# Thirteen gate projections of the first feed-forward as seven products on half the tokens instead of eight

## Chip, cores and metric

One NeuronCore of one Trainium2 chip runs the whole program in one launch. The metric is device microseconds of one execution, the median of three. Everything is in 32-bit floats; where a matmul operand is split into two parts, the parts are `float32r`, the engine's reduced 32-bit type.

## The reference

One inference step of one decoder layer on 256 prompt tokens and 8 x 8 sample tokens, 320 tokens together, with a model width of 2048:

```python
x += 0.5 * swiglu(rmsnorm(x, ln_ffa), w_ffa_in, w_ffa_out)   # first feed-forward, D_FF = 5632
x += token_mixer(rmsnorm(x, ln_mix), ...)                    # mLSTM and dilated attention
x += 0.5 * swiglu(rmsnorm(x, ln_ffb), w_ffb_in, w_ffb_out)   # second feed-forward
y = rmsnorm(x, ln_f)

def swiglu(x, w_in, w_out):
    gate, up = jnp.split(x @ w_in, 2, axis=-1)
    return (jax.nn.silu(gate) * up) @ w_out
```

The change concerns `x @ w_in` of the first feed-forward, gate half. New keys, values and recurrent states are outputs too.

## The kernel before

Channels lie on the 128 partitions and tokens in the free dimension, so a matmul has a 128 x 128 piece of the weights as stationary operand and a channel tile of 128 x 320 (NT = 320 tokens) as moving operand. For accuracy, both operands are split into a high and a low part, and each product is three matmuls: high weight by high data (`xh,hi`), high weight by low data (`xl,hi`), low weight by high data (`xh,lo`). Each of these matmuls loads its own weights first.

The matmuls are cut into jobs, one for each 256 output channels, and a job into chunks of up to four channel tiles. A chunk's weights (128 x 4 x 256, 512 KB) come by one DMA into a `raw` tile (5 buffers); ScalarE copies `raw` to `hi` (L239), VectorE writes `lo` = `raw` - `hi` (L112 is the helper through which all of VectorE's instructions pass); `hi` and `lo` have 3 buffers each (HLB = 3). A full chunk is 4 tiles x 2 column halves x 3 = 24 matmuls (L147 is the helper that issues them).

The program's order is written out by hand, per chunk, at its head in `run_job`: postponed work first (`run_later`: what `later(...)` was given at the chunk before), then in a job's first chunk the evacuation of the job before (`flush_evac`), then `split_upto(ci + HLB)`, which splits the weights of the chunk two places ahead into the buffers that the chunk before this one used, then one step of the background generators (`step`), the loads, and last the chunk's matmuls. Each engine takes its instructions strictly in this order.

The first feed-forward has 22 pairs of jobs, in blocks of 6, 6, 5 and 5. Each pair is a gate job (16 channel tiles, 4 chunks, 96 matmuls) and an up job of the same size. After a block come 8 jobs that multiply by `w_ffa_out`. A gate job's PSUM tile is evacuated in the up job's first chunk: VectorE multiplies by `rstd` into `gt`, ScalarE applies SiLU, GpSimd multiplies by `rstd` again (L472). An up job's PSUM tile is evacuated in the next job's first chunk: VectorE multiplies it by `gt` into `hf`, ScalarE copies that to `hh`, VectorE writes `hl`; these are the moving operands of the `w_ffa_out` jobs. `fg` tiles (2 banks, 2 buffers) hold the PSUM of the jobs, `bg` tiles (1 bank, 4 buffers) the small work. The first gate and up job run in a start-up routine of their own, with the same 192 matmuls.

Of the kernel before, what the change touches and what calls it, by code (L numbers as in the profile page):

```python
# [9 lines left out]
F32 = mybir.dt.float32  # L10
# [112 lines left out]
def decoder_kernel(tc, I, O, K):  # L123
# [54 lines left out]
    def run_later(force=False):  # L178
        run_queue(later_q, force)
# [38 lines left out]
    def split_upto(n):  # L218
        while st["split"] < min(n, len(chunks)):
            i = st["split"]  # L220
            load_upto(i + 1)
            src, nk, kind = chunks[i]
            hi = wp.tile([128, 4, 256], F32R, tag="hi", bufs=HLB, name="hi")
            lo = wp.tile([128, 4, 256], F32R, tag="lo", bufs=HLB, name="lo")
            t = raw.pop(i)
            if kind == "mif":
                r = t.rearrange("p a b -> p (a b)")[:, :128].rearrange("p (k c) -> p k c", k=16)
                pair = []
                for a, w in enumerate((hi, lo)):
                    G.memset(w.bitcast(F32), 0.0)  # L230
                    x = w.rearrange("p a b -> p (a b)").rearrange("p (k c) -> p k c", k=8)
                    for o, s in ((0, 0), (32, 4)):
                        rk = r[:, 8 * a:8 * a + 8, s:s + 4]
                        S.copy(x[:, :, o:o + 4], rk)
                        V.tensor_tensor(x[:, :, o + 64:o + 68], rk, x[:, :, o:o + 4].bitcast(F32), op=OP.subtract)
                    pair.append(x)
                wh[i], wl[i] = pair, None
            else:
                S.copy(hi[:, :nk], t[:, :nk])  # L239
                V.tensor_tensor(lo[:, :nk], t[:, :nk], hi[:, :nk].bitcast(F32), op=OP.subtract)  # L240
                wh[i], wl[i] = hi, lo
            st["split"] += 1
# [17 lines left out]
                k += nk  # L260
        jobs.append((cs, nkt, mov, evac, kind, setup))

    fgps = [0]

    def fg_tile():
        return pp.tile([128, 2, 512], F32, tag="fg", bufs=2, name="fg")
# [7 lines left out]
    def flush_evac():  # L274
        if pending:
            evac, ps = pending.pop(0)
            g = evac(ps)
            if g is not None:
                try:
                    next(g)  # L280
                    every.append(g)
                except StopIteration:
                    pass

    def run_job(job):
        cs, nkt, mov, evac, kind, setup = job
        third = cs[0][0] == 8
        ps = [bg_tile(), bg_tile()] if third else fg_tile()
        for n, (ci, k0, nk) in enumerate(cs):
            us = CHUNK_US + extra[0]  # L290
            V.next_chunk(us)
            moved[1] = max(0.0, moved[1] + moved[0] - us * MB_PER_US)
            extra[0] = moved[0] = 0.0
            run_later()
            now = list(every)
            if n == 0 and setup is not None:
                setup()
            if n == (3 if third else 0) or ci == 13:
                flush_evac()
            split_upto(ci + HLB)  # L300
            run_queue(soon_q)
            if tick[0] % 2 == 0:
                step(even)
                if moved[1] < 3.4:
                    step(slow)
            else:
                step(odd)
            tick[0] += 1
            step(every, now)
            while fill and V.has_room(CHUNK_US + extra[0]):  # L310
                if next(fill[0], True):
                    break
            load_upto(ci + HLB + RAWB)
            h, l = wh.pop(ci), wl.pop(ci)
            if kind == "mif":
                for k in range(nk):
                    for n2, x in enumerate(mov(k0 + k)):
                        mm(ps[:, 0, 0:NT], h[k // 8][:, k % 8], x, start=k == 0 and n2 == 0, stop=k == nk - 1 and n2 == 1)
                continue
            for m in range(2):  # L320
                for k in range(nk):
                    if ci == 10 and m == 0 and k == 2:
                        rstd_now(True)
                    xh, xl = mov(k0 + k)
                    a, b = h[:, k, m * 128:(m + 1) * 128], l[:, k, m * 128:(m + 1) * 128]
                    out = ps[m][:, 0:NT] if third else ps[:, m, 0:NT]
                    first, last = k0 + k == 0, k0 + k == nkt - 1
                    mm(out, a, xh, start=first, stop=False)
                    mm(out, a, xl, start=False, stop=False)
                    mm(out, b, xh, start=False, stop=last)  # L330
        pending.append((evac, ps))

    def drain(n=100000):
        while (every or even or odd or slow) and n > 0:
# [125 lines left out]
        S.copy(h, xe)  # L460
        V.tensor_tensor(l, xe, h.bitcast(F32), op=OP.subtract)

    def ff_jobs(w_in, w_out, get, last_evac, first_setup=None):
        f0 = 0
        for bi, nb in enumerate(FF_BLOCKS):
            for m in range(0, nb, 2):
                def gate_evac(ps):
                    p = get()
                    gt = p.tile([128, 2, NT], F32, tag="ft", bufs=4, name="gt")
                    times_rstd(gt, ps)  # L470
                    S.activation(gt, gt, AF.Silu)  # L471
                    G.tensor_tensor(gt, gt, bcast(rstd, 2), op=OP.mult)  # L472
                    state["gt"] = gt

                def up_evac(ps, m=m):
                    p = get()
                    h = p.tile([128, 2, NT], F32, tag="ft", bufs=4, name="hf")
                    V.tensor_tensor(h, ps[:, :, 0:NT], state["gt"], op=OP.mult)
                    hh = p.tile([128, 2, NT], F32R, tag="h", bufs=state["hb"], name="hh")
                    hl = p.tile([128, 2, NT], F32R, tag="h", bufs=state["hb"], name="hl")  # L480
                    split(h, hh, hl)
                    H_H[m // 2], H_L[m // 2] = hh, hl

                add_job(w_in, 0, 16, (f0 + m) * 128, mov_x, gate_evac,
                        setup=first_setup if (bi == 0 and m == 0) else None)
# [21 lines left out]

    state["hb"] = 12
    pool_box = {"p": fp}
    ff_jobs(I["w_ffa_in"], I["w_ffa_out"], lambda: pool_box["p"], ffa_last)  # L510
    n_ffa = len(jobs)


# [1221 lines left out]
    spawn(init_tables(), even)  # L1735
    run_start()
    spawn(first_sumsq())
    for job in jobs[2:-1]:
        run_job(job)
    run_last(jobs[-1])  # L1740
# [129 lines left out]
```

## Time and profile before

| | |
|---|---|
| median of three runs | 2663.82 us (2663.71 to 2666.66) |
| the profiled execution's own time | 2665.36 us |
| its span | 2663.4 us |
| TensorE matmul busy / weight load busy | 99% / 99% of the span, 21296 instructions each |
| VectorE, ScalarE, GpSimd busy | 57%, 43%, 6% |
| granted TensorE clock | 0.998 of full speed |

A row of the profile's groups reads: line, engine, operation, written tile <- read tiles, shapes, count | busy time in all, mean ns of one | idle time of the engine before them and who ended it. PE is the matmul queue, PEld the weight loads, which the profile records as separate instructions; matmuls overlap, so their durations are longer than the distance from one to the next. DVE is VectorE, ACT ScalarE, POOL GpSimd. A row of the timeline reads: start, duration of the merged instructions, then the same names.

### The profile page before, as it was taken

The numbers are of one execution on the slowest core, as the hardware profiler recorded it, in microseconds if no ns is written. First come the engines' busy times: TensorE is split into PE (matmuls) and PEld (weight loads), VectorE is DVE, ScalarE is ACT, GpSimd is POOL, SyncE is SP. The second block draws the span as 40 slices with busy tenths as digits, with TensorE's granted clock in tenths as the row PEclk, the third lists the DMA queues.
The fourth block names the chain that finished last, engine by engine and source line by source line (L and its number), as shares of the span: only waits on it lengthen the run. The fifth ranks groups of instructions, "written<-read, shape, count | busy, mean of one in ns | idle before, by whom it ended". The sixth has DMA issues, their size and how long they took to land.

```text
span 2663.4 us, 50949 instructions
## 1 busy us (share of the span) xinstructions
PE 2647.3 (99%) x21296; PEld 2629.3 (99%) x21296; DVE 1518.3 (57%) x1962; ACT 1136.1 (43%) x1879; POOL 147.5 (6%) x171
## 2 busy tenths in 40 slices
PE   9999999999999999999999999999999999999998
PEld 9999999999999999999999999999999999999998
DVE  6444444444446576777766656655545555554445
ACT  6333333333334455555544445443333433433334
POOL 0000000000000000111101000000000000000000
PEclk9999999999999999999999999999999999999999
DMA  6544455445546778899999876566666565555444
GB/s 238 161 164 163 163 159 165 159 155 163 168 159 186 248 245 296 310 343 324 339 375 355 319 257 228 192 201 201 195 203 194 176 214 187 194 168 174 160 152 132
DMA packets 202290, 571.55 MB, mean 215 GB/s; under 512 B 23488, under 2 KB 65096, under 8 KB 202060
## 3 DMA queue, kind: packets, MB, share of 16 engines
q1 hardware_dynamic: 201340, 566.99, 63.4%
q8 instruction: 166, 2.72, 0.4%
q10 hardware_dynamic: 720, 1.31, 0.1%
q14 instruction: 64, 0.52, 0.1%
HBM read 535.45 MB, written 32.78 MB: 213 GB/s over the span
## 4 chain that ended last, share of the span: by engine, by line
PE 98%; DMA 1%; DVE 0%; ACT 0%; SPq 0%; issue 0%; DVEq 0%; ACTq 0%
PE fg L147 93%; PE bg L147 4%; DMA vt<-in_old_v_dram 1%; PE bg L357 1%; DMA fk<-in_far_k_dram 0%; DMA x<-in_x_t_dram 0%; DVE x L112 0%; DVE lo L112 0%; SPq L139 0%; DVE rows L112 0%; ACT xh L1653 0%; ACT hi L239 0%; ACT lg L1747 0%; ACT hi L1643 0%; ACT s L604 0%
## 5 line engine op out<-in xcount | busy, mean ns | idle before, releaser
L112 DVE TENSOR_TENSOR lo<-raw,hi 128x1024 fp32r<-128x1024 f32 (+2 forms) x794 | 966.4, 1222 | 847.6 <-ACT hi L239 827.6
L147 PE MATMUL fg<-xh,hi 128*128 128x320 f32 x4200 | 1258.4, 301 | 1.4 <-ACT hi L1643 1.4
L147 PE MATMUL fg<-xh,lo 128*128 128x320 f32 x4200 | 1248.3, 299 | 0.3 <-DVE lo L112 0.3
L147 PE MATMUL fg<-xl,hi 128*128 128x320 f32 x4200 | 1248.3, 299 | 0.0
L239 ACT CAST hi<-raw 128x1024 fp32r<-128x1024 f32 (+1 forms) x776 | 793.2, 1026 | 1062.6 <-PE fg L147 899.6
L147 PEld LDWEIGHTS fg<-xh,hi 128*128 128x128 f32 x4200 | 791.5, 189 | 7.4 <-issue 2.9
L147 PEld LDWEIGHTS fg<-xl,hi 128*128 128x128 f32 x4200 | 791.8, 189 | 0.6
L147 PEld LDWEIGHTS fg<-xh,lo 128*128 128x128 f32 x4200 | 791.4, 189 | 0.6 <-DVE lo L112 0.6
L147 PE MATMUL fg<-hh,hi 128*128 128x320 f32 x1408 | 421.4, 299 | 0.0
L147 PE MATMUL fg<-hl,hi 128*128 128x320 f32 x1408 | 421.0, 299 | 0.0
L147 PE MATMUL fg<-hh,lo 128*128 128x320 f32 x1408 | 421.0, 299 | 0.0
L147 PEld LDWEIGHTS fg<-hh,hi 128*128 128x128 f32 x1408 | 266.1, 189 | 0.3
L147 PEld LDWEIGHTS fg<-hl,hi 128*128 128x128 f32 x1408 | 266.1, 189 | 0.1
L147 PEld LDWEIGHTS fg<-hh,lo 128*128 128x128 f32 x1408 | 266.1, 189 | 0.0
L472 POOL TENSOR_TENSOR gt<-gt,rstd 128x640 f32<-128x640 f32 x44 | 68.2, 1549 | 1651.5 <-ACT gt L471 1651.5
L147 PE MATMUL fg<-bh,hi 128*128 128x320 f32 x512 | 153.3, 299 | 0.0
L147 PE MATMUL fg<-bl,hi 128*128 128x320 f32 x512 | 153.1, 299 | 0.0
L147 PE MATMUL fg<-bh,lo 128*128 128x320 f32 x512 | 153.1, 299 | 0.0
L147 PEld LDWEIGHTS fg<-bh,hi 128*128 128x128 f32 x512 | 96.8, 189 | 0.2 <-issue 0.2
L147 PEld LDWEIGHTS fg<-bl,hi 128*128 128x128 f32 x512 | 96.8, 189 | 0.0
L147 PEld LDWEIGHTS fg<-bh,lo 128*128 128x128 f32 x512 | 96.8, 189 | 0.0
L460 ACT CAST hh<-hf 128x640 fp32r<-128x640 f32 x44 | 34.8, 790 | 143.5 <-DVE hf L112 143.5
(264 smaller groups left out, 1414.7 us busy)
## 6 DMA issues: line engine op xcount, KB each, us to landing
raw<-in_w_in_dram SPq DMA_DIRECT2D x176, 512.0 KB
raw<-in_w_ffb_in_dram SPq DMA_DIRECT2D x176, 512.0 KB
raw<-in_w_ffa_in_dram SPq DMA_DIRECT2D x171, 512.0 KB
raw<-in_w_ffa_out_dram SPq DMA_DIRECT2D x80, 512.0 KB
vt<-in_old_v_dram SPq DMA_DIRECT2D x80, 512.0 KB
raw<-in_w_ffb_out_dram SPq DMA_DIRECT2D x80, 512.0 KB
fk<-in_far_k_dram SPq DMA_DIRECT2D x48, 512.0 KB
nk<-in_near_k_dram SPq DMA_DIRECT2D x32, 512.0 KB
```

The lines of the kernel that those rows point to most:

```text
L112: return fn(*a, **k)
L147: T.matmul(out, a, b, start=start, stop=stop, **kw)
L239: S.copy(hi[:, :nk], t[:, :nk])
L357: T.transpose(out, in_, ident[:k, :k])
L460: S.copy(h, xe)
L472: G.tensor_tensor(gt, gt, bcast(rstd, 2), op=OP.mult)
```

## The change

In pairs 3, 4, 6, 7, 9, 10, 12, 13, 15, 16, 18, 19 and 21 (counted from 0) the gate and the up job become one job of kind `pair`, whose eight chunks alternate gate, up, gate, up. The up chunks compute what they did, into two `bg` tiles. A gate chunk is computed by a seven-product scheme for 2 x 2 block matrices: two channel tiles by two column halves of the weights, times two channel tiles by two halves of the tokens (HT = 160). A block takes 7 products of 128 x 128 by 128 x 160, each again three matmuls, so 42 matmuls a chunk and 168 a gate job. Four of the seven weight operands are sums and differences of weight tiles: VectorE forms them from `raw` (tiles `f` and `g`, named `sums`), ScalarE and VectorE split them into `sh` and `sl`. Four of the seven moving operands are sums of token halves; `token_sums` forms them once (`th`, `tl`), as a background generator during pairs 1 and 2. The seven products accumulate in an `fg` tile and a `bg` tile; `gate_evac7` and `join7` add them up into `gt`. The head of a chunk becomes a function (`head`), the plain matmuls another (`plain`); both are the code of `run_job` moved, and `split_upto` gets a branch for kind `s`.

```diff
+            elif kind == "s":
+                sh, sl = (pool_box["p"].tile([128, 4, 2, 128], F32R, tag=g, bufs=2, name=g) for g in ("sh", "sl"))
+                f, g = (t_tile(F32, "sums").rearrange("p m n -> p (m n)")[:, 0:512].rearrange("p (q b n) -> p q b n", q=2, b=2)
+                        for _ in range(2))
+                S.copy(hi, t)
+                V.tensor_tensor(f.rearrange("p q b n -> p b q n"), raw_ap(t, 128, [[t.ap[0][0], 128], [512, 2], [0, 2], [1, 128]]),
+                                raw_ap(t, 0, [[t.ap[0][0], 128], [512, 2], [384, 2], [1, 128]]), op=OP.add)
+                V.tensor_tensor(g[:, 0], f[:, 1], t[:, 0::2, 0:128], op=OP.add)
+                V.tensor_tensor(g[:, 1], g[:, 0], t[:, 1::2, 0:128], op=OP.add)
+                for n, x in ((0, f), (2, g)):
+                    S.copy(sh[:, n:n + 2], x)
+                for k in (slice(0, 4), slice(1, 4, 2)):
+                    c = slice(0, 128) if k.start == 0 else slice(128, 256)
+                    V.tensor_tensor(lo[:, k, c], t[:, k, c], hi[:, k, c].bitcast(F32), op=OP.subtract)
+                for n, x in ((0, f), (2, g)):
+                    V.tensor_tensor(sl[:, n:n + 2], x, sh[:, n:n + 2].bitcast(F32), op=OP.subtract)
+                wh[i], wl[i] = (hi, sh), (lo, sl)
...
+    def add_pair(w, k_all, c0, c1, mov, evac0, evac1):
+        cs = []
+        for k in range(0, k_all, 4):
+            for a, c in enumerate((c0, c1)):
+                cs.append((len(chunks), k, a))
+                chunks.append((wsrc(w, k, 4, c), 4, "w" if a else "s"))
+        jobs.append((cs, k_all, mov, (evac0, evac1), "pair", None))
...
+    HT = NT // 2
+
+    def run_pair(job):
+        cs, nkt, mov, evac, kind, setup = job
+        f = fg_tile()
+        g = bg_tile()
+        acc = [g[:, 0:HT] if b == 0 else f[:, b - 1, c * HT:(c + 1) * HT] for b, _, c in
+               ((0, 0, 0), (1, 0, 0), (1, 0, 2), (2, 0, 0), (2, 0, 1), (1, 0, 1), (2, 0, 2))]
+        opens = (0, 1, 3)
+        u = None
+        for n, (ci, k0, a) in enumerate(cs):
+            hl = head(ci, 1 if n not in (0, 7) else 0)
+            if a:
+                if u is None:
+                    u = [bg_tile(), bg_tile()]
+                plain([t[:, 0:NT] for t in u], hl, mov, k0, 4, nkt)
+            else:
+                assert state["sums"]
+                (h, sh), (l, sl) = hl
+                for b in range(2):
+                    j = (k0 + 2 * b) // 2
+                    x = [tuple(t[j][:, kk].rearrange("p (j i) -> p i j", j=2)[:, 80 * c:80 * c + 80] for t in (XH, XL))
+                         for kk, c in ((0, 0), (1, 0), (1, 1))]
+                    y = [tuple(t[j][:, q // 2].rearrange("p (j i) -> p i j", j=2)[:, 80 * (q % 2):80 * (q % 2) + 80]
+                               for t in (TH, TL)) for q in range(4)]
+                    k = 2 * b
+                    w = [(t[:, k, 0:128], t[:, k + 1, 0:128], None, t[:, k + 1, 128:256]) for t in (h, l)]
+                    v = [[t[:, q, b] for q in range(4)] for t in (sh, sl)]
+                    left = [(w[0][0], w[1][0]), (w[0][1], w[1][1]), (v[0][3], v[1][3]), (w[0][3], w[1][3]),
+                            (v[0][1], v[1][1]), (v[0][2], v[1][2]), (v[0][0], v[1][0])]
+                    right = [x[0], x[1], x[2], y[3], y[0], y[1], y[2]]
+                    first, last = k0 + b == 0, k0 + k == nkt - 2
+                    for i, ((p, q), (xh, xl)) in enumerate(zip(left, right)):
+                        mm(acc[i], p, xh, start=first and i in opens, stop=False)
+                        mm(acc[i], p, xl, start=False, stop=False)
+                        mm(acc[i], q, xh, start=False, stop=last and b and i in (0, 5, 6))
+            if n == 6:
+                pending.append((evac[0], (f, g)))
+        pending.append((evac[1], u))
...
+    TH, TL = {}, {}
+
+    def join7(o, f):
+        o = o.rearrange("p m n -> p (m n)").rearrange("p (s n) -> p s n", s=4)
+        p, q = (f[:, b, 0:3 * HT].rearrange("p (s n) -> p s n", s=3) for b in range(2))
+        p34 = raw_ap(f, 2 * HT, [[f.ap[0][0], 128], [512 - 2 * HT, 2], [1, HT]])
+        V.tensor_tensor(o[:, 0::3], o[:, 0::3], p[:, 0:2], op=OP.add)
+        V.tensor_tensor(o[:, 1], o[:, 3], q[:, 1], op=OP.subtract)
+        V.tensor_tensor(o[:, 2], q[:, 2], o[:, 3], op=OP.subtract)
+        V.tensor_tensor(o[:, 3], o[:, 2], q[:, 1], op=OP.add)
+        V.tensor_tensor(o[:, 1:3], o[:, 1:3], p34, op=OP.add)
+
+    def token_sums(gcol):
+        for j in range(8):
+            x, t = t_tile(F32, "tx"), t_tile(F32, "tf")
+            for m in range(2):
+                S.activation(x[:, m], X[j][:, m], AF.Copy, scale=gv[:, gcol + 2 * j + m:gcol + 2 * j + m + 1])
+            t4 = t.rearrange("p m n -> p (m n)").rearrange("p (s n) -> p s n", s=4)
+            a, b = ([x[:, m, c * HT:(c + 1) * HT] for c in range(2)] for m in range(2))
+            yield
+            V.tensor_tensor(t4[:, 0], a[1], a[0], op=OP.subtract)
+            V.tensor_tensor(t4[:, 2], a[1], b[1], op=OP.subtract)
+            V.tensor_tensor(t4[:, 1], t4[:, 0], b[1], op=OP.subtract)
+            V.tensor_tensor(t4[:, 3], t4[:, 1], b[0], op=OP.add)
+            TH[j], TL[j] = (pool_box["p"].tile([128, 2, NT], F32R, tag="tt", bufs=16, name=n) for n in ("th", "tl"))
+            src = [t4[:, 2 * i:2 * i + 2].rearrange("p b (i j) -> p j b i", j=2) for i in range(2)]
+            hi, lo = ([u[:, i].rearrange("p (j b i) -> p j b i", j=2, b=2) for i in range(2)] for u in (TH[j], TL[j]))
+            for i in range(2):
+                S.copy(hi[i], src[i])
+            yield
+            for i in range(2):
+                V.tensor_tensor(lo[i], src[i], hi[i].bitcast(F32), op=OP.subtract)
+        state["sums"] = True
...
+                def gate_evac7(ps):
+                    gt = get().tile([128, 2, NT], F32, tag="ft", bufs=4, name="gt")
+                    S.copy(gt.rearrange("p m n -> p (m n)").rearrange("p (s n) -> p s n", s=4)[:, 0::3], bcast(ps[1][:, 0:HT], 2))
+
+                    def rest():
+                        join7(gt, ps[0])
+                        V.tensor_tensor(gt, gt, bcast(rstd, 2), op=OP.mult)
+                        S.activation(gt, gt, AF.Silu)
+                        G.tensor_tensor(gt, gt, bcast(rstd, 2), op=OP.mult)
+                        state["gt"] = gt
+
+                    later(rest)
+
                 def up_evac(ps, m=m):
                     p = get()
                     h = p.tile([128, 2, NT], F32, tag="ft", bufs=4, name="hf")
-                    V.tensor_tensor(h, ps[:, :, 0:NT], state["gt"], op=OP.mult)
+                    if isinstance(ps, list):
+                        for i in range(2):
+                            V.tensor_tensor(h[:, i], ps[i][:, 0:NT], state["gt"][:, i], op=OP.mult)
+                    else:
+                        V.tensor_tensor(h, ps[:, :, 0:NT], state["gt"], op=OP.mult)
                     hh = p.tile([128, 2, NT], F32R, tag="h", bufs=state["hb"], name="hh")
                     hl = p.tile([128, 2, NT], F32R, tag="h", bufs=state["hb"], name="hl")
                     split(h, hh, hl)
                     H_H[m // 2], H_L[m // 2] = hh, hl
 
+                if seven(f0 + m):
+                    add_pair(w_in, 16, (f0 + m) * 128, DFF + (f0 + m) * 128, mov_x, gate_evac7, up_evac)
+                    continue
...
-    ff_jobs(I["w_ffa_in"], I["w_ffa_out"], lambda: pool_box["p"], ffa_last)
+    ff_jobs(I["w_ffa_in"], I["w_ffa_out"], lambda: pool_box["p"], ffa_last, seven=lambda m: m >= 6 and m // 2 % 3 != 2)
...
     spawn(first_sumsq())
+    spawn(token_sums(G_FFA))
```

On TensorE, the start of the gate job of pair 3. Before (`xh`, `xl`: the two parts of the moving data; `hi`, `lo`: of the weights; `fg`: PSUM):

```order
L147 MATMUL fg<-xh,hi 128x320 [waits Activation_49]
L147 MATMUL fg<-xl,hi 128x320
L147 MATMUL fg<-xh,lo 128x320 [waits DVE_49]
L147 MATMUL fg<-xh,hi 128x320
L147 MATMUL fg<-xl,hi 128x320
L147 MATMUL fg<-xh,lo 128x320
```

After (`sh`, `sl`: the parts of the weight sums; `th`, `tl`: of the token sums):

```order
L147 MATMUL bg<-xh,hi 128x160 [waits Activation_49]
L147 MATMUL bg<-xl,hi 128x160
L147 MATMUL bg<-xh,lo 128x160 [waits DVE_49]
L147 MATMUL fg<-xh,hi 128x160 [waits PE_49]
L147 MATMUL fg<-xl,hi 128x160
L147 MATMUL fg<-xh,lo 128x160
L147 MATMUL fg<-xh,sh 128x160 [waits Activation_49]
L147 MATMUL fg<-xl,sh 128x160
L147 MATMUL fg<-xh,sl 128x160 [waits DVE_49]
L147 MATMUL fg<-th,hi 128x160
L147 MATMUL fg<-tl,hi 128x160
L147 MATMUL fg<-th,lo 128x160
```

The matmuls are half as wide and more; the third product also waits for `sh` and `sl`.

On VectorE, from the evacuation of a gate job to the first weights split after the up job. Before (`lo`: low part of a chunk's weights, one row a chunk):

```order
L112 TENSOR_TENSOR gt<-fg,rstd 128x640 [waits PE_49]
L112 TENSOR_TENSOR lo<-raw,hi 128x1024 [waits DMAHW4_49,DVE_49,Activation_49]
L112 TENSOR_TENSOR lo<-raw,hi 128x1024 [waits DVE_49,DMAHW5_49,PE_49,Activation_49]
L112 TENSOR_TENSOR lo<-raw,hi 128x1024 [waits DVE_49,DMAHW6_49,PE_49,Activation_49]
L112 TENSOR_TENSOR lo<-raw,hi 128x1024 [waits DMAHW7_49,PE_49,Activation_49]
L112 TENSOR_TENSOR hf<-fg,gt 128x640 [waits PE_49,Pool_49]
L112 TENSOR_TENSOR hl<-hf,hh 128x640 [waits Activation_49]
L112 TENSOR_TENSOR lo<-raw,hi 128x1024 [waits DMAHW0_49,Activation_49]
```

After, between pairs 3 and 4:

```order
L112 TENSOR_TENSOR gt<-gt,fg 128x2x160 [waits PE_49]
L112 TENSOR_TENSOR gt<-gt,fg 128x160 [waits DVE_49]
L112 TENSOR_TENSOR gt<-fg,gt 128x160
L112 TENSOR_TENSOR gt<-gt,fg 128x160 [waits DVE_49]
L112 TENSOR_TENSOR gt<-gt,fg 128x320 [waits DVE_49]
L112 TENSOR_TENSOR gt<-gt,rstd 128x640 [waits DVE_49]
L112 TENSOR_TENSOR hf<-bg,gt 128x320 [waits PE_49,Pool_49]
L112 TENSOR_TENSOR hf<-bg,gt 128x320 [waits PE_49]
L112 TENSOR_TENSOR hl<-hf,hh 128x640 [waits Activation_49]
L112 TENSOR_TENSOR sums<-raw 128x2x2x128 [waits DMAHW0_49]
L112 TENSOR_TENSOR sums<-sums,raw 128x256 [waits DVE_49] x2
L112 TENSOR_TENSOR lo<-raw,hi 128x4x128 [waits Activation_49]
```

Four chunks' splits stood between the making of `gt` and its use in `hf`; now none does, and the weights of the chunk two places on come behind both.

More of the change, by code (lines that the diff above doesn't have):

```diff
@@ L261, in add_job @@
         jobs.append((cs, nkt, mov, evac, kind, setup))
-    fgps = [0]
+    def add_pair(w, k_all, c0, c1, mov, evac0, evac1):
[5 more added lines that the diff above has]
+        jobs.append((cs, k_all, mov, (evac0, evac1), "pair", None))
     def fg_tile():
@@ L283, in flush_evac, with head, plain @@
                     pass
+    def head(ci, n, third=False, setup=None):
+        us = CHUNK_US + extra[0]
+        V.next_chunk(us)
+        moved[1] = max(0.0, moved[1] + moved[0] - us * MB_PER_US)
+        extra[0] = moved[0] = 0.0
+        run_later()
+        now = list(every)
+        if n == 0 and setup is not None:
+            setup()
+        if n == (3 if third else 0) or ci == 13:
+            flush_evac()
+        split_upto(ci + HLB)
+        run_queue(soon_q)
+        if tick[0] % 2 == 0:
+            step(even)
+            if moved[1] < 3.4:
+                step(slow)
+        else:
+            step(odd)
+        tick[0] += 1
+        step(every, now)
+        while fill and V.has_room(CHUNK_US + extra[0]):
+            if next(fill[0], True):
+                break
+        load_upto(ci + HLB + RAWB)
+        return wh.pop(ci), wl.pop(ci)
+    def plain(outs, hl, mov, k0, nk, nkt, at=None):
+        h, l = hl
+        for m in range(2):
+            for k in range(nk):
+                if at == (m, k):
+                    rstd_now(True)
+                xh, xl = mov(k0 + k)
+                a, b = h[:, k, m * 128:(m + 1) * 128], l[:, k, m * 128:(m + 1) * 128]
+                first, last = k0 + k == 0, k0 + k == nkt - 1
+                mm(outs[m], a, xh, start=first, stop=False)
+                mm(outs[m], a, xl, start=False, stop=False)
+                mm(outs[m], b, xh, start=False, stop=last)
     def run_job(job):
         cs, nkt, mov, evac, kind, setup = job
+        if kind == "pair":
+            run_pair(job)
+            return
         third = cs[0][0] == 8
@@ L289, in run_job @@
         for n, (ci, k0, nk) in enumerate(cs):
[L290 to L314, printed above, removed]
+            hl = head(ci, n, third, setup)
             if kind == "mif":
+                h, l = hl
                 for k in range(nk):
@@ L319, in run_job @@
                 continue
[L320 to L330, printed above, removed]
@@ L331, in run_job @@
-        pending.append((evac, ps))
+            outs = [ps[m][:, 0:NT] if third else ps[:, m, 0:NT] for m in range(2)]
+            plain(outs, hl, mov, k0, nk, nkt, (0, 2) if ci == 10 else None)
+        pending.append((evac, ps))
+    HT = NT // 2
[36 more added lines that the diff above has]
+        pending.append((evac[1], u))
@@ L461, in split, with ff_jobs @@
         V.tensor_tensor(l, xe, h.bitcast(F32), op=OP.subtract)
-    def ff_jobs(w_in, w_out, get, last_evac, first_setup=None):
+    TH, TL = {}, {}
[11 more added lines that the diff above has]
+            x, t = t_tile(F32, "tx"), t_tile(F32, "tf")
+            for m in range(2):
+                S.activation(x[:, m], X[j][:, m], AF.Copy, scale=gv[:, gcol + 2 * j + m:gcol + 2 * j + m + 1])
[15 more added lines that the diff above has]
+        state["sums"] = True
+    def ff_jobs(w_in, w_out, get, last_evac, first_setup=None, seven=lambda m: False):
         f0 = 0
@@ L477, in up_evac @@
                     h = p.tile([128, 2, NT], F32, tag="ft", bufs=4, name="hf")
-                    V.tensor_tensor(h, ps[:, :, 0:NT], state["gt"], op=OP.mult)
+                    if isinstance(ps, list):
+                        for i in range(2):
+                            V.tensor_tensor(h[:, i], ps[i][:, 0:NT], state["gt"][:, i], op=OP.mult)
+                    else:
+                        V.tensor_tensor(h, ps[:, :, 0:NT], state["gt"], op=OP.mult)
                     hh = p.tile([128, 2, NT], F32R, tag="h", bufs=state["hb"], name="hh")
```

## The prediction

> **What bounds the kernel now.** I read the page first, then the chain of work that ended last, then the groups of instructions by shape, then the timeline at a few places.
>
> ```profile
> span 2663.4 us, 50949 instructions
> PE 2647.3 (99%) x21296; PEld 2629.3 (99%) x21296; DVE 1518.3 (57%) x1962; ACT 1136.1 (43%) x1879; POOL 147.5 (6%) x171
> PE 98%; DMA 1%; DVE 0%; ACT 0%; SPq 0%; issue 0%; DVEq 0%; ACTq 0%
> ```
>
> TensorE is the bound from end to end. The chain by pieces gives its pace, and a window over most of the first feed-forward gives the others' load there:
>
> ```profile
> 46.98 831.30 PE fg L147 x6120
> 60.00:720.00 660.00, 660.00 (x4861) 660.00 (x4860) 316.71 (x282) 235.65 (x241) 27.93 (x18) 1.00 0.50 162
> ```
>
> The first row is 831.30 / 6120 = 0.1358 us from one 320-column matmul to the next, or 0.424 ns a column, without a break. The second lists PE, PEld, DVE, ACT and POOL busy, the clock (1.00) and the DMA share: VectorE is busy 48% and ScalarE 36% of this stretch. So what the change does to TensorE's pace counts in full, and work on the others counts only where it comes late.
>
> Every matmul loads 128 columns of weights first. The groups by shape give the records' durations, for split matmuls and their loads, plain 32-bit ones (`q,k`) and transposes (`ident`):
>
> ```profile
> L147 PE MATMUL fg<-xh,hi 128*128 128x320 f32 x4200 | 1258.4, 301 | 1.4 <-ACT hi L1643 1.4
> L147 PE MATMUL bg<-q,k 128*128 128x256 f32 x16 | 4.1, 379 | 0.0
> L147 PE MATMUL bg<-q,k 128*128 128x128 f32 x16 | 2.4, 274 | 0.0
> L357 PEld LDWEIGHTS bg<-ident,s 128*128 128x128 f32 x24 | 2.9, 141 | 0.7 <-ACT s L610 0.3 <-ACT s L611 0.3
> L147 PEld LDWEIGHTS fg<-xl,hi 128*128 128x128 f32 x4200 | 791.8, 189 | 0.6
> ```
>
> At 320 columns the load is hidden. How long it takes shows where it isn't:
>
> ```profile
> 970.76 0.19 PEld L147 LDWEIGHTS fg<-xh,hi 128*128 128x128 f32 x1
> 970.77 0.40 PE L147 MATMUL fg<-xh,hi 128*128 128x320 f32 x1
> 970.87 0.19 PEld L147 LDWEIGHTS fg<-xl,hi 128*128 128x128 f32 x1
> ...
> 1214.46 0.30 PEld L147 LDWEIGHTS bg<-qn,ones 128*128 128x128 f32 x2
> 1214.51 0.39 PE L147 MATMUL bg<-qn,ones 128*128 128x64 f32 x2
> 1214.68 0.73 PEld L147 LDWEIGHTS bg<-z,vh 128*128 128x128 f32 x4
> 1214.74 0.76 PE L147 MATMUL bg<-z,vh 128*128 128x256 f32 x3
> ```
>
> At 970.76 the queue had run empty. The first split matmul's load started, the second's 0.11 us later, and the first matmul took 0.40 us where the group's mean is 0.301: it stood 0.10 us for its own weights. At 1214.46 the matmuls have only 64 columns: two loads take 0.22 us, two matmuls 0.23. So a matmul with full weights of its own cannot follow the last in less than about 0.112 us (0.110 to 0.115), however narrow it is. The 64-column ones are plain 32-bit, the first are `float32r` as in the change; both say 0.11.
>
> **The products, step by step.** A gate job now is 96 x 0.1358 = 13.04 us. After, it is 168 matmuls of 160 columns. Streamed at 0.424 ns a column they would take 0.068 us each, 11.41 us, 1.63 less. At the load's 0.112 they take 18.82 us, 5.78 more. The change breaks even at 13.04 / 168 = 0.0776 us. I take the load's 0.112: 13 x 5.78 = **+75 us**. The far ends: -21 us (streamed), and the price of plain 32-bit matmuls, should narrow ones fall back to it. Those appear twice in the records (8 products, x16), and 128 more columns cost each record 379 - 274 = 105 ns, so 160 columns cost 2 x 160 x 0.82 = 0.263 us: 13 x (44.2 - 13.04) = +405 us. No row ties split matmuls to that price. The up chunks keep 24 x 0.1358 = 3.26 us each; a gate chunk becomes 42 x 0.112 = 4.70 us.
>
> The Trainium skill speaks for another pace: "TensorE: Matmul & The Clock Gate", section "Back-to-back issue gap", gives a sustained 81 ns for load and matmul at 128 columns and 131 ns at 512; between them an estimate for 160 is 85 ns, which would make the sum 13 x (14.3 - 13.04) = +16 us. The trace disagrees: 0.11 us at 64 columns.
>
> **The sums of weights.** Rows nearest in size, the first from the timeline:
>
> ```profile
> 116.47 1.23 DVE L112 TENSOR_TENSOR lo<-raw,hi 128x1024 fp32r<-128x1024 f32 x1 [0.32 <-ACT hi L239]
> L112 DVE TENSOR_TENSOR lo<-raw,hi 128x512 fp32r<-128x512 f32 x46 | 31.2, 686 | 8.7 <-ACT hi L239 6.6 <-ACT hi L1643 2.2
> L112 DVE TENSOR_TENSOR lo<-raw,hi 128x256 fp32r<-128x256 f32 x4 | 1.7, 424 | 1.7 <-ACT hi L1643 1.7
> L112 DVE TENSOR_TENSOR gt<-bg,rstd 128x320 f32<-128x320 f32 x2 | 0.9, 480 | 0.0
> L112 DVE TENSOR_TENSOR s<-bg,tp 128x128 f32<-128x128 f32 x8 | 2.2, 273 | 0.0
> L239 ACT CAST hi<-raw 128x512 fp32r<-128x512 f32 x32 | 19.6, 614 | 8.7 <-PE fg L147 8.7
> L471 ACT ACTIVATE gt<-gt 128x640 f32<-128x640 f32 x44 | 32.4, 737 | 138.1 <-DVE gt L112 138.1
> L472 POOL TENSOR_TENSOR gt<-gt,rstd 128x640 f32<-128x640 f32 x44 | 68.2, 1549 | 1651.5 <-ACT gt L471 1651.5
> ```
>
> A gate chunk's split on VectorE was one instruction of 1.23 us. Now it is 0.69 (`f`), 2 x 0.42 (`g`), 0.69 + 0.42 (`lo`), 2 x 0.69 (`sl`), 4.0 us; ScalarE adds 2 x 0.61. Against a gate chunk of 4.70 us and an up chunk of 3.26 (VectorE 1.23) both fit, hidden behind the matmuls: no cost in mid-job. A whole pair is 25.3 us of VectorE, evacuations included, beside 31.9 us of TensorE. Without that cover (streamed matmuls, 24.5 us a pair) VectorE would be the bound by about 1 us a pair. `token_sums` is about 18 us each of VectorE and ScalarE, spread over the 52 us of pairs 1 and 2 with VectorE half idle: nothing, at worst 18 us. Weight bytes and DMAs stay as they are; a `raw` tile is held some 3 us longer out of a five-chunk lead: nothing.
>
> **The new wait at the end of a pair.** Here is the end of an up job now (its last matmul ends at about 112.2), VectorE and then ScalarE:
>
> ```profile
> 112.29 0.82 DVE L112 TENSOR_TENSOR hf<-fg,gt 128x640 f32<-128x640 f32 x1 [1.16 <-PE fg L147]
> 113.97 0.83 DVE L112 TENSOR_TENSOR hl<-hf,hh 128x640 fp32r<-128x640 f32 x1 [0.86 <-ACT hh L460]
> 114.92 1.22 DVE L112 TENSOR_TENSOR lo<-raw,hi 128x1024 fp32r<-128x1024 f32 x1
> ...
> 113.15 0.79 ACT L460 CAST hh<-hf 128x640 fp32r<-128x640 f32 x1 [3.28 <-DVE hf L112]
> 113.84 1.04 ACT L239 CAST hi<-raw 128x1024 fp32r<-128x1024 f32 x1
> ```
>
> Call that end T. The split two chunks ahead is ready at T + 3.9 and TensorE needs it at T + 6.5: 2.6 us to spare. After the change the chain that makes `gt` stands in front. From T - 3.26, when the last up chunk begins: ScalarE copies the first product (0.79, as `hh`) and casts a `hi` (1.04), VectorE writes its `lo` (1.23), then joins (2 x 0.48 + 3 x 0.31, the last between the 128- and 256-wide rows) and multiplies by `rstd` (0.83, as `hl`): T + 2.6. SiLU 0.74 and GpSimd 1.55: T + 4.9, and until then VectorE and all splits queued behind `hf` stand still. `hf` 2 x 0.48, `hh` 0.79, `hl` 0.83, handoffs 0.2: T + 7.7. Then the split:
> - Before another seven-product job (6 times) it needs `f`, `g`, `lo`, `sl`, 4.0 us, T + 11.7; TensorE is there at T + 4.70 + 3.26, and at the third product 0.9 later, T + 8.9: 2.8 us late.
> - Before a plain gate job (5 times): 1.23 after ScalarE's `hi`, T + 9.2, needed at its third matmul at T + 6.8: 2.4 us late.
> - Before `w_ffa_out` jobs of ten tiles (2 times) the third chunk is half as long: T + 8.5, 1.7 us late.
>
> That is 6 x 2.8 + 5 x 2.4 + 2 x 1.7 = **+32 us**. The trace has no such wait; the bounds are nothing (if a seven-product split starts while `hf` waits) and about 48 us (joins and handoffs half as slow again). The order of instructions has VectorE stopped at `hf`, so I keep 32. Evacuating earlier is worth nothing elsewhere.
>
> Sum: 75 + 32 = 107 us. The profiled execution took 2663.4 us in its span and 2665.36 in all, 1.5 us above the median, so on the median's footing 2663.8 + 107 gives **2771 us**.
>
> **Rivals.**
> - Faster: the loads hide behind narrow matmuls (0.068 us each) and the boundary waits are covered, 2663.8 - 21 = 2643 us. It decides if the pace falls under 0.0776 us and the waits stay under 1.6 us a pair. For it: the load's record, 189 ns, is no bound at 320 columns; against it, the two places with 0.11 us. 3%.
> - Streamed, but VectorE cannot follow: TensorE is at the third product at T + 6.7, 5.0 us late at six boundaries, so waits of 6 x 5.0 + 15.4 = 45 us outweigh 21: 2688 us. 5%.
> - Loads of another kind, between both paces: the transposes' 128-column loads (`ident`, 141 ns against 189) show that a quicker load exists. Halfway, 0.090 us, is 13 x (15.12 - 13.04) = +27, with waits of 39 us: 2730 us. 6%. The skill's 85 ns, above, would be here.
> - The load's pace, but the boundary waits hidden: 2739 us. 10%.
> - The plain 32-bit price: +405 and waits of 15 us, 3084 us. 6%.
>
> **How the numbers follow.** The forecast has 70%: paces of 0.108 to 0.116 us give +66 to +84 us, waits of 20 to 48 us come on top, so 2750 to 2796. The range reaches down to take in the hidden waits and most of the middle pace, 2728 to 2802; it leaves out the first two rivals and the last, 14%, and a few per cent of the edges. Faster by over 0.2% (what a measurement of this kernel can tell from no change): the first rival and a corner of the second, 4%. Within 0.2%: 1%. Slower: 95%.
>
> **What would show it.** In the changed kernel's profile, matmuls of 128x160 start 0.11 us apart, in groups with weight loads back to back; the 13 `pair` jobs take about 32 us, and a gate chunk 4.7. TensorE gets idle time of 1.5 to 3.5 us once per pair, ended by VectorE (`lo` or `sl`), in the chunk two after the up job; VectorE's idle time before `hf` is ended by GpSimd. Outside the first feed-forward nothing moves. I am wrong if the 160-column matmuls start less than 0.1 us or more than 0.13 us apart, or if TensorE's idle time stays at a few us.

## The result, and the profile after

The kernel before took 2663.77 us (median of four runs, 2662.93 to 2666.66), the changed one 2753.89 us (2751.03 to 2756.41): a ratio of 1.0337, with a 95% interval of 1.0324 to 1.0350. It is 90 us slower. The four executions of the changed kernel took 2751.03, 2751.63, 2756.14 and 2756.41 us; the last is the profiled one, and the accounts below are made on its trace. From the page of the changed kernel, its span, the engines' busy times and the engines' shares of the chain that ended last:

```profile
span 2754.6 us, 53383 instructions
PE 2730.4 (99%) x22232; PEld 2709.5 (98%) x22232; DVE 1675.4 (61%) x2400; ACT 1210.7 (44%) x2028; POOL 146.5 (5%) x171
PE 94%; DVE 3%; ACT 1%; POOL 0%; issue 0%; DMA 0%; SPq 0%; DVEq 0%; ACTq 0%; POOLq 0%
```

TensorE remains the bound, now with 936 more matmuls (13 x 72), and VectorE has entered the chain with 3%. The groups of the changed kernel by shape, one that waits for nothing and the one that ends a block's third product and can wait for `sl`, give the new matmuls and their idle time:

```profile
L147 PE MATMUL fg<-th,sl 128*128 128x160 f32 x312 | 86.7, 278 | 0.0
L147 PE MATMUL fg<-xh,sl 128*128 128x160 f32 x104 | 29.2, 281 | 4.5 <-DVE sl L112 4.5
```

Half the columns take 278 ns in the records where 320 took 301: the records' durations hardly fall. What counts is the distance from one to the next. The timeline of TensorE at the start of pair 6 in the kernel before and, in the second fence, in the changed one (and the first matmuls of pairs 7 and 8):

```profile
242.42 0.30 PE L147 MATMUL fg<-xh,hi 128*128 128x320 f32 x1
242.55 0.30 PE L147 MATMUL fg<-xl,hi 128*128 128x320 f32 x1
...
268.50 0.30 PE L147 MATMUL fg<-xh,hi 128*128 128x320 f32 x1
```

```profile
265.61 0.23 PE L147 MATMUL bg<-xh,hi 128*128 128x160 f32 x1
265.68 0.28 PE L147 MATMUL bg<-xl,hi 128*128 128x160 f32 x1
265.79 0.28 PE L147 MATMUL bg<-xh,lo 128*128 128x160 f32 x1
265.90 0.28 PE L147 MATMUL fg<-xh,hi 128*128 128x160 f32 x1
...
297.41 0.23 PE L147 MATMUL bg<-xh,hi 128*128 128x160 f32 x1
...
330.11 0.30 PE L147 MATMUL fg<-xh,hi 128*128 128x320 f32 x1
```

Apart from the first, which comes 0.07 us before its successor, the narrow matmuls start 0.11 us apart (the median over all 2184 of them is 112 ns; the 320-column ones keep 136). Pair 6 takes 297.41 - 265.61 = 31.80 us where it took 268.50 - 242.42 = 26.08: 5.72 us more. Pair 7 takes 32.70, which is the same 31.80 and 0.9 us of waiting in its third chunk, nearly all at the third product; pair 8, a plain one, waits 0.63 in its third chunk. The first feed-forward ends at 961.42 us instead of 868.34, 93.1 us later. By the pairs' first matmuls in the two traces:

| where | us later |
|---|---|
| 13 pairs with seven products, 5.72 each | 74.4 |
| waits in the third chunk of six such pairs that follow another (0.88) and of five plain pairs that follow one (0.63) | 8.5 |
| `token_sums` in pairs 0 to 2 (-0.1, +2.6, +0.8) | 3.3 |
| pair 3, beyond its 5.72 | 6.9 |

These make the 93.1. What follows the first feed-forward takes 2 us less than before, so the span grows by 91.2. Of these, 1.8 us are one wait of TensorE for a DMA, which the trace of the kernel before has and that of the changed one hasn't. Among the experiments below some traces have it (2.0 us in the fifth) and most don't, so it isn't the change's doing.

### The profile page after: what moved, and what is told of

Same layout as the page of the kernel before. It is cut to its first block, busy times and chain, and to the rows that moved or that the text cites. A ratio compares the mean times of both kernels' runs of the same rounds, so it can differ in the third digit from the quotient of the medians.

```text
span 2754.6 us, 53383 instructions
## 1 busy us (share of the span) xinstructions
PE 2730.4 (99%) x22232; PEld 2709.5 (98%) x22232; DVE 1675.4 (61%) x2400; ACT 1210.7 (44%) x2028; POOL 146.5 (5%) x171
## 4 chain that ended last, share of the span: by engine, by line
PE 94%; DVE 3%; ACT 1%; POOL 0%; issue 0%; DMA 0%; SPq 0%; DVEq 0%; ACTq 0%; POOLq 0%
PE fg L147 84%; PE bg L147 10%; DVE lo L112 1%; PE bg L431 1%; DVE gt L112 1%; ACT hi L256 0%; DVE sums L112 0%; DVE sl L112 0%; POOL gt L591 0%; DVE hf L112 0%; DVE hl L112 0%; ACT hh L534 0%; DMA x<-in_x_t_dram 0%; DVE x L112 0%; ACT gt L590 0%
## 5 line engine op out<-in xcount | busy, mean ns | idle before, releaser
L147 PE MATMUL fg<-xh,hi 128*128 128x320 f32 (+1 forms) x3472 | 1038.2, 301 | 2.1 <-ACT hi L1771 1.9
L147 PE MATMUL fg<-xh,lo 128*128 128x320 f32 (+1 forms) x3472 | 1029.3, 299 | 4.1 <-DVE lo L112 4.1
L147 PE MATMUL fg<-xl,hi 128*128 128x320 f32 (+1 forms) x3472 | 1028.1, 298 | 0.0
L147 PEld LDWEIGHTS fg<-xh,hi 128*128 128x128 f32 x3472 | 654.4, 189 | 7.9 <-issue 2.9
L147 PEld LDWEIGHTS fg<-xh,lo 128*128 128x128 f32 x3472 | 654.2, 189 | 6.6 <-DVE lo L112 6.5
L147 PEld LDWEIGHTS fg<-xl,hi 128*128 128x128 f32 x3472 | 654.5, 189 | 0.6
L147 PE MATMUL bg<-xh,lo 128*128 128x320 f32 (+1 forms) x552 | 163.7, 297 | 0.7 <-DVE lo L112 0.7
L147 PE MATMUL bg<-xh,hi 128*128 128x320 f32 (+1 forms) x552 | 163.9, 297 | 0.0
L147 PE MATMUL bg<-xl,hi 128*128 128x320 f32 (+1 forms) x552 | 163.6, 296 | 0.0
L147 PEld LDWEIGHTS bg<-xh,lo 128*128 128x128 f32 x552 | 105.5, 191 | 0.9 <-DVE lo L112 0.9
```

Of the source, the lines that this page charges most:

```text
L147: T.matmul(out, a, b, start=start, stop=stop, **kw)
```

## The experiments

**The narrow matmuls alone.** The kernel before, with the matmuls of the same 13 gate jobs cut in two halves of the tokens: no sums, no joins.

```diff
+                    if kind == "half":
+                        for c in range(2):
+                            o, yh, yl = out[:, 160 * c:160 * c + 160], xh[:, 80 * c:80 * c + 80], xl[:, 80 * c:80 * c + 80]
+                            mm(o, a, yh, start=first and c == 0, stop=False)
+                            mm(o, a, yl, start=False, stop=False)
+                            mm(o, b, yh, start=False, stop=last and c == 1)
+                        continue
...
```

> The kernel before, with one part of the change alone: the same 13 gate jobs as plain eight-product jobs, but each matmul cut into two on 160 tokens, 192 matmuls instead of 96, no sums at all. Load theory (each matmul cannot follow in less than the 0.112 us that its 128-column weight load takes): 13 x (192 x 0.112 - 13.04) = +110 us, 2774 us. Rival, columns alone count (0.424 ns each) and the change's time came from its sums and waits: no change, 2664 us.

It took 2773.75 us (2772.75 to 2774.89), 1.0415 of the kernel before (1.0398 to 1.0433): +110 us for 1248 more matmuls. Timeline of TensorE in this kernel, three neighbours of a gate job:

```profile
267.74 0.28 PE L147 MATMUL fg<-xh,hi 128*128 128x160 f32 x1
267.85 0.28 PE L147 MATMUL fg<-xl,hi 128*128 128x160 f32 x1
267.96 0.28 PE L147 MATMUL fg<-xh,lo 128*128 128x160 f32 x1
```

Again 0.11 us (median 112 ns), with nothing of the scheme but the width. So the pace belongs to the 160-column matmul with its own weights, not to VectorE's sums.

**Half the weight columns, then half the moving columns.** In the changed kernel, six of each job's eight blocks use 64 weight columns, or else 80 moving columns. The two edits differ in one line; both are shown, and the comments are not in the code.

```diff
+                        o = acc[i]
+                        if 0 < k0 + b < 13:
+                            o, p, q = o[0:64], p[:, 0:64], q[:, 0:64]               # the first kernel
+                            o, xh, xl = o[:, 0:80], xh[:, 0:40], xl[:, 0:40]        # the second, instead
...
```

> The changed kernel, with the weights of six of the eight blocks of every seven-product gate job cut to 64 columns (half of those outputs is left out); 1638 matmuls load 64 columns instead of 128 and move the same 160 columns. Load theory: they fall from 0.112 to about 0.07 us, -69 us less what VectorE then holds up, 2685 to 2715 us. Rival, a narrow matmul costs 0.112 us whatever it loads: 2754 us.

> The changed kernel, with the moving data of six of the eight blocks of every seven-product gate job cut from 160 to 80 columns (half of those tokens is left out), loads as they were. Load theory: 0.112 us as before, 2754 us within 3. Rival, the cost goes by columns, 0.112 / 160 us each: 1638 x 0.056 = -92 us, 2662 us.

The first took 2694.41 us (2693.76 to 2695.07; ratio 1.0116, 1.0096 to 1.0136), the second 2795.92 (2791.89 to 2799.94; 1.0497, 1.0476 to 1.0518). Timeline of TensorE, first the 64-column weights, then the 80-column data:

```profile
290.63 0.23 PE L147 MATMUL fg<-th,lo 128*64 128x160 f32 x1
290.70 0.23 PE L147 MATMUL fg<-th,sh 128*64 128x160 f32 x1
290.77 0.23 PE L147 MATMUL fg<-tl,sh 128*64 128x160 f32 x1
```

```profile
291.17 0.28 PE L147 MATMUL fg<-xh,sh 128*128 128x80 f32 x1
291.28 0.28 PE L147 MATMUL fg<-xl,sh 128*128 128x80 f32 x1
291.39 0.28 PE L147 MATMUL fg<-xh,sl 128*128 128x80 f32 x1
```

With half the load the pace falls to 0.07 us (median 69 ns, the 160 columns' own 0.424 ns each); with half the data it stays at 0.11 (median 112). That settles the load as the bound of the narrow matmuls. The time of the second kernel is a miss all the same: 42 us over the changed kernel, where the load theory had none. A window over the first feed-forward (after PE, PEld, DVE, ACT and POOL stands the granted clock), of the changed kernel and then of this one:

```profile
60.00:960.00 900.00, 892.61 (x6897) 889.63 (x6896) 552.87 (x793) 370.27 (x459) 32.65 (x22) 0.99 0.47 148
```

```profile
60.00:960.00 900.00, 892.36 (x6653) 889.64 (x6652) 530.34 (x764) 352.95 (x434) 32.67 (x22) 0.96 0.44 140
```

The clock is 0.96 against 0.99: it fell to half again and again, for 3.4 to 10.2 us (from 100.2, 141.1, 311.8, 322.0, 373.2 us and on), and there the narrow matmuls stand 0.21 us apart. These falls make nearly all of the miss: over the first feed-forward they add up to 78.5 us, in which 103 narrow steps took 0.213 instead of 0.112 us and 209 wide ones 0.267 instead of 0.136, a loss of 38 us, against 5 us in the changed kernel's single fall; and the first feed-forward ends 32.7 us later in the one trace than in the other. The load theory held for the pace and said nothing of the clock.

**No sums of weights.** Parts of `hi` and `lo` stand in for the split sums, and the split is the plain one.

```diff
-                sh, sl = (pool_box["p"].tile([128, 4, 2, 128], F32R, tag=g, bufs=2, name=g) for g in ("sh", "sl"))
...
-                for n, x in ((0, f), (2, g)):
-                    V.tensor_tensor(sl[:, n:n + 2], x, sh[:, n:n + 2].bitcast(F32), op=OP.subtract)
+                V.tensor_tensor(lo, t, hi.bitcast(F32), op=OP.subtract)
+                sh, sl = (w.rearrange("p (b k) (r n) -> p (k r) b n", b=2, r=2) for w in (hi, lo))
```

> The changed kernel without the sums of weights: each gate chunk is split as a plain chunk, and parts of its hi and lo stand in for the sums (the result is not the reference's). VectorE has 1.23 us a gate chunk instead of 4.0. Load theory: 42 matmuls still take 4.70 us; only the waits before a following seven-product job (6 x 0.9) and part of the 7 us at pair 3 go, 2743 to 2749 us. Rival, VectorE's and ScalarE's extra work sets the pace: -80 us, about 2674 us.

2751.66 us (2751.36 to 2754.01), ratio 1.0333 (1.0318 to 1.0348): above the 2743 to 2749 expected. The pairs still take 31.80 us, so VectorE's 4 us a chunk aren't the pace. The wait between two seven-product pairs falls from 0.88 to 0.2, but before a plain pair it grows from 0.63 to 1.59, and 0.85 appears before the two groups of `w_ffa_out` jobs. ScalarE at the end of pair 6 in this kernel says why (a timeline; in brackets the idle time and who ended it):

```profile
285.18 0.43 ACT L573 COPY gt<-bg 128x320 f32<-128x320 f32 x1 [1.78 <-PE bg L147]
287.02 1.05 ACT L244 CAST hi<-raw 128x1024 fp32r<-128x1024 f32 x1 [1.42 <-PE fg L147]
```

Here `sh` is part of `hi`, so a chunk's last products read `hi` to the chunk's end, and the next `hi` waits 1.42 us for them. The evacuation's chain starts later by that. Pair 3 takes 31.80 us here too, though `token_sums` runs and pairs 1 and 2 lose their 3.4 us as before: the waits of pair 3 need both kinds of sums together.

**The join without the postponement.**

```diff
-                    later(rest)
+                    rest()
```

> The changed kernel, with the joining of the seven products, SiLU and GpSimd's multiplication issued in the last up chunk, ahead of its weights' split, instead of one chunk later ahead of the up job's evacuation. Theory (VectorE stands at hf until GpSimd has made gt, and the next splits come late): gt is ready some 0.8 us or more earlier, so the wait of 0.88 us at each of six boundaries falls under 0.3 and that of 0.63 us at five goes, -5 to -8 us, 2746 to 2749 us. Rival, the length of the following split alone makes the wait: six waits of about 0.9 us stay, 2751 to 2754 us.

2756.61 us (2749.84 to 2757.86), ratio 1.0338 (1.0321 to 1.0356): no gain in the median, where 5 to 8 us were expected. The waits only went from 0.88 to 0.77 and from 0.63 to 0.52, 1.2 us in all. The median hides even these: three of the four executions lie at 2756 to 2758 us with a mean clock of 0.996 or 0.997, the profiled one among them, with a fall of 10.2 us in pair 3; the fourth, at 0.999, took 2749.84, where the changed kernel's two at 0.998 took 2751.03 and 2751.63. VectorE and GpSimd in this kernel at pair 7:

```profile
298.87 1.80 DVE L112 TENSOR_TENSOR lo<-raw,hi 128x1024 fp32r<-128x1024 f32 x1 [1.74 <-ACT hi L256]
300.59 0.88 DVE L112 TENSOR_TENSOR hf<-bg,gt 128x320 f32<-128x320 f32 x2
```

```profile
298.05 1.54 POOL L591 TENSOR_TENSOR gt<-gt,rstd 128x640 f32<-128x640 f32 x1 [120.29 <-ACT gt L590]
```

`gt` was ready at 299.6, but `hf` starts at 300.59, as late as in the changed kernel (300.76). The `lo` ahead of it on VectorE had to wait for a `hi` that now stood behind SiLU on ScalarE, and it took 1.80 us instead of 1.23, beside GpSimd's instruction.

**No sums of tokens.** The data's own halves stand in for them; `token_sums` isn't run.

```diff
-                               for t in (TH, TL)) for q in range(4)]
+                               for t in (XH, XL)) for q in range(4)]
...
-    spawn(token_sums(G_FFA))
+    state["sums"] = True
```

> The changed kernel without token_sums: halves of the data stand in for the sums as moving operands (the result is not the reference's). Theory (the sums crowd VectorE and ScalarE in pairs 1 to 3): pair 1 loses its 2.6 us, pair 2 its 0.8 and pair 3 its 7.0 over the 5.7 of the products, -10 us, 2744 us. Rival, pair 3's 7.0 us belong to the first change from plain to seven products: only -3.4 us, 2750 us.

2746.58 us (2746.48 to 2747.62), ratio 1.0310 (1.0295 to 1.0325). Pairs 1 and 2 are back at 26.62 and 26.08 us, pair 3 takes 31.80 instead of 38.75, and the later waits stay. In the trace the first feed-forward ends 10.2 us earlier, which is all that the table gives to `token_sums` and pair 3. Some 5 us of it belong to the fall of the clock that the changed kernel's profiled execution has in pair 3 (below): against its two executions at clock 0.998 the gain is 4.8 us.

**The join ahead of the split, SiLU behind it.** Join and product with `rstd` run at once; `soon` puts SiLU and GpSimd's step behind the chunk's split.

```diff
+                    join7(gt, ps[0])
+                    V.tensor_tensor(gt, gt, bcast(rstd, 2), op=OP.mult)
+
                     def rest():
-                        join7(gt, ps[0])
-                        V.tensor_tensor(gt, gt, bcast(rstd, 2), op=OP.mult)
...
-                    later(rest)
+                    soon(rest)
```

> The changed kernel, with the join of the seven products issued in the last up chunk ahead of its weights' split, and SiLU and GpSimd's multiplication behind that split. In the run that joined at once, hf started no earlier (300.59 instead of 300.76) because the split's hi stood behind SiLU on ScalarE and its lo behind the join and beside GpSimd's instruction (1.80 us instead of 1.23). Theory: with hi ahead of SiLU, hf starts about 1.3 us earlier, which is more than the 0.88 and 0.63 us of the waits: they go, -8 us against the changed kernel. Rival, the split's own length makes them: they stay above 0.5 us each.

2744.88 us (2742.91 to 2747.89), ratio 1.0307 (1.0291 to 1.0322), 9 us under the changed kernel, or 8 if the executions at a clock of 0.998 or more are compared (2742.91 and 2743.41 here, 2751.03 and 2751.63 there). All eleven later waits are gone: each pair takes 31.80 or 26.08 us. VectorE's `hf` at pair 7 (whose first matmul starts at 294.15 here):

```profile
296.50 0.89 DVE L112 TENSOR_TENSOR hf<-bg,gt 128x320 f32<-128x320 f32 x2 [1.44 <-POOL gt L592]
```

That is T + 2.35 us instead of T + 3.35: one microsecond clears the boundary. In the profiled execution pair 3 still takes 37.1 us.

**The same, with the token sums' four adds on GpSimd.**

```diff
-            V.tensor_tensor(t4[:, 0], a[1], a[0], op=OP.subtract)
+            G.tensor_tensor(t4[:, 0], a[1], a[0], op=OP.subtract)
...
```

> As the run before, and token_sums forms its sums on GpSimd instead of VectorE. Theory (VectorE is crowded in pairs 1 to 3, and the two waits in pair 3 bring the clock down to half for 10 us): pairs 1 and 2 lose less than half of their 3.4 us, the waits in pair 3 fall under 0.5 us each, the clock stays at 1.00 and pair 3 takes about 32 us instead of 38.8; with the boundaries that leaves the products' +74 us and 1 to 3 us more, 2738 to 2742 us. Rival, pair 3 waits for its token sums or ScalarE, not for VectorE's share of them: pair 3 stays above 33 us.

2742.17 us (2741.65 to 2742.35), ratio 1.0295 (1.0278 to 1.0312). The time is just over the upper edge of what was expected, and the way there came true only in part: pairs 1 and 2 keep 3.2 us (1.7 and 1.5), and pair 3 keeps two waits, 0.4 and 0.6 us of idle time. Its clock doesn't fall, and it takes 33.28 us, which is above the 33 that the rival named. ScalarE shows what the adds on GpSimd left as it was in pair 1:

```profile
58.82 1.10 ACT L565 CAST th<-tf 128x320 fp32r<-128x320 f32 x2 [3.16 <-POOL tf L559]
```

The next `hi` stands behind this `th` on ScalarE, and the next `lo` waits for that `hi`. Against the two executions of the seventh experiment without a fall (2742.91 and 2743.41) the move gains 1 us; all four executions here have a clock of 0.998 or 0.999. This is the best version with seven products that was run, and it is 78 us slower than the kernel before: the products' 74 us and 4 more.

## Why the prediction was right, and where not

**The products: right.** +75 us was forecast from 0.112 us a matmul, read where the queue had run empty and at 64-column matmuls; 74.4 was found, at 112 ns. The streamed rivals fall with it. Eight products of the same width (the first experiment) show the same pace, 64-column weights break it and 80-column data don't. The rival of a quicker load, at 0.090, falls too, and so does the plain 32-bit price. The estimate of 85 ns from the Trainium skill's "TensorE: Matmul & The Clock Gate", section "Back-to-back issue gap", isn't met by `float32r` with 128 weight columns; the trace has 112.

**The waits at the end of a pair: mechanism right, size wrong.** 32 us were forecast, 8.5 were measured: 0.88 instead of 2.8, 0.63 instead of 2.4, nothing instead of 1.7. ScalarE and VectorE of the changed kernel at the end of pair 6, whose successor's first matmul is at T = 297.41:

```profile
292.35 0.42 ACT L585 COPY gt<-bg 128x320 f32<-128x320 f32 x1 [0.70 <-PE bg L147]
293.24 1.05 ACT L256 CAST hi<-raw 128x1024 fp32r<-128x1024 f32 x1 [0.46 <-PE fg L147]
```

```profile
294.32 1.23 DVE L112 TENSOR_TENSOR lo<-raw,hi 128x1024 fp32r<-128x1024 f32 x1 [1.44 <-ACT hi L256]
...
297.44 0.82 DVE L112 TENSOR_TENSOR gt<-gt,rstd 128x640 f32<-128x640 f32 x1
...
300.76 0.89 DVE L112 TENSOR_TENSOR hf<-bg,gt 128x320 f32<-128x320 f32 x2 [2.49 <-POOL gt L591]
...
305.71 1.28 DVE L112 TENSOR_TENSOR sl<-sums,sh 128x512 fp32r<-128x512 f32 x2
```

The working started the chain with the last up chunk, at T - 3.26 = 294.15. In the trace both ScalarE steps stand ahead of it: the copy takes 0.42 us (it moves 320 elements, and the row taken for it had 640) and is done before that chunk, and `hi` starts at 293.24, 0.9 us early, because the gate chunk ahead reads its `hi` for the last time with ten matmuls (1.1 us) still to come. So `hf` begins at T + 3.35 instead of T + 4.9, and the last `sl` ends at T + 9.6 instead of T + 11.7. The fourth experiment, where `hi` is read to the chunk's end, gets part of the forecast back: `hf` at T + 4.3 there (294.54, T = 290.23), 1.59 us before a plain pair and 0.85 before `w_ffa_out`. What is late and who waits came out as told, in the changed kernel's TensorE at both kinds of boundary:

```profile
306.13 0.28 PE L147 MATMUL fg<-xl,sh 128*128 128x160 f32 x1
307.05 0.34 PE L147 MATMUL fg<-xh,sl 128*128 128x160 f32 x1 [0.64 <-DVE sl L112]
...
337.43 0.40 PE L147 MATMUL fg<-xh,lo 128*128 128x320 f32 x1 [0.36 <-DVE lo L112]
```

The third product of pair 7 comes 0.92 us after its neighbour instead of 0.11, and a plain pair waits for `lo`. A wait worked out as the difference of two long chains carries the error of every step in them: with hardly any step off by more than a microsecond, it came out three to four times too long. The seventh experiment shows that it was about a microsecond from nothing, which is the rival of hidden boundary waits; the measured 2754 us lies as near to that rival's 2739 as to the 2771 forecast.

**`token_sums`: forecast nothing, "at worst 18 us"; 10.2 us were measured in the profiled execution.** "VectorE half idle" was true of pair 2 before the change (13.23 of its 26.08 us busy) and less of pair 1 (17.16 of 26.62). The step that failed is the one from room on an engine to no cost. Windows over pairs 1 and 2 and the start of pair 3 in the changed kernel:

```profile
35.00:63.00 28.00, 25.95 (x184) 24.83 (x182) 19.15 (x34) 17.56 (x29) 3.09 (x2) 1.00 0.46 149
63.00:90.00 27.00, 26.96 (x198) 26.73 (x198) 22.43 (x41) 16.51 (x27) 3.21 (x2) 1.00 0.51 157
89.00:97.00 8.00, 8.00 (x67) 7.91 (x67) 6.46 (x13) 4.70 (x8) 0.00 (x0) 1.00 0.47 134
100.00:104.00 4.00, 4.00 (x22) 4.00 (x22) 3.91 (x7) 1.53 (x3) 0.00 (x0) 0.58 0.54 179
104.00:108.00 4.00, 4.00 (x19) 4.00 (x19) 3.60 (x7) 1.08 (x2) 0.00 (x0) 0.50 0.59 207
```

VectorE is busy 83% of pair 2, but only 68% of the first window, where most of the 3.4 us of pairs 1 and 2 are lost. So VectorE's load alone isn't the cause. At the last of these waits it is the order of instructions: on ScalarE a `hi` comes behind a `th`, which waits for VectorE's sums, and VectorE then stands idle for that `hi`. ScalarE, VectorE and TensorE there:

```profile
59.89 0.89 ACT L565 CAST th<-tf 128x320 fp32r<-128x320 f32 x2 [2.50 <-DVE tf L112]
60.69 1.04 ACT L256 CAST hi<-raw 128x1024 fp32r<-128x1024 f32 x1
61.76 1.23 DVE L112 TENSOR_TENSOR lo<-raw,hi 128x1024 fp32r<-128x1024 f32 x1 [1.54 <-ACT hi L256]
63.04 0.40 PE L147 MATMUL fg<-xh,lo 128*128 128x320 f32 x1 [0.31 <-DVE lo L112]
```

In pair 3, where VectorE also has the weights' sums, come two waits of some 0.85 us each beyond the normal distance. TensorE's timeline there:

```profile
98.44 0.34 PE L147 MATMUL bg<-xh,lo 128*128 128x160 f32 x1 [0.75 <-DVE lo L112]
...
99.98 0.34 PE L147 MATMUL fg<-xh,sl 128*128 128x160 f32 x1 [0.65 <-DVE sl L112]
...
101.01 0.42 PE L147 MATMUL fg<-th,sh 128*128 128x160 f32 x1
101.22 0.42 PE L147 MATMUL fg<-tl,sh 128*128 128x160 f32 x1
```

Then, from 100.6 to 110.8 us, the granted clock is 0.50, the matmuls stand 0.21 us apart, and some 5 us more are lost. Without `token_sums`, or without the sums of weights, neither these two waits nor the fall occur. The runs of the changed kernel lie at 2751 (clock 0.998) and at 2756 us (0.997, the profiled one among them), which fits a fall that comes in some executions; only the profiled one can be looked into.

**The forecast as a whole.** 2771 was forecast and 2754 measured, inside the range of 2728 to 2802. Two errors of opposite sign, -23.5 us at the boundaries and +10.2 at the token sums, made the sum look better than its terms; the rest of the program's 2 us is most of the remainder. That it came out within the 2750 to 2796 of the forecast itself is luck: the products' 74.4 us and the boundaries' 8.5 alone give 2746.7, and the token sums, priced at nothing, lift it over 2750. It was to be wrong if the 160-column matmuls started under 0.1 or over 0.13 us apart: they don't. The other sign, TensorE's idle time staying at a few us, comes closer: TensorE's idle time that VectorE ended rose from 0.3 to 9.3 us, and no boundary has the 1.5 to 3.5 us that were to be seen once per pair.

## What to carry to other kernels

A `float32r` matmul that loads its own weights had two bounds here, its moving columns and its load, and fewer multiplications help only while the columns are the larger: 160 columns (0.068 us) fell under a 128-column load (0.112), so seven products of half the width cost more than eight of full width. Count a scheme in matmuls times the larger bound before costing its sums. A short preparation beside a tight stretch is to be costed by the order of the queues that it stands in, since an engine with room left can still be late with what the next one needs.

## What the runs showed of the hardware

- **The clock falls without an idle stretch.** Two waits of under a microsecond, 1.5 us apart among narrow matmuls, stood just ahead of 10.2 us at half clock; 80-column matmuls brought falls over and over. Falls last 3.4, 6.8 or 10.2 us. "TensorE: Matmul & The Clock Gate" of the Trainium skill, Part 1, has a window of about 3.4 us after whose idleness the clock halves: the length agrees with these falls, but TensorE's queue was never empty that long here.
- **What decides is how much streams, as far as these traces go.** The 13 falls of the 80-column kernel start whole multiples of 3.41 us after one another (12, 62, 65 and 80 of them after the first, and on). Cut the first feed-forward of all ten traces, from 30 us on, into windows on that grid (each trace has a fall at its end that fixes it), and count each matmul's columns at 0.424 ns: an estimate of the share of a window in which columns stream. The 17 falls there each follow a window with a share of 0.16 to 0.38; the 2625 windows at full clock that no fall follows have 0.397 or more. Narrow matmuls alone have 0.068 / 0.112 = 0.61 at 160 columns and 0.30 at 80. With its two waits the changed kernel's window has 0.31, and the last experiment's, where the first wait is shorter, 0.43. This was found in the traces afterwards; no run was made to test it.
- **VectorE beside GpSimd.** A VectorE subtraction of two operands in SBUF took 1.80 us instead of 1.23 while a GpSimd instruction ran. The Trainium skill's "SBUF — State Buffer", section "Who interferes with whom", says that such an instruction reads its second operand through an interface shared with GpSimd, and that the one which starts later stands still until the other is done. The trace agrees to 0.15 us: 1.23 us counted from GpSimd's end (299.59) would end at 300.82, and it ended at 300.67.
- **Changes of width.** The first 160-column matmul after wide ones is followed after 0.07 us, not 0.11, as if its successor's load had been done behind it; the first 320-column one after narrow ones after 0.18 us instead of 0.136 (294.11 to 294.29 us in the changed kernel).
